# Row vectors loaded by GpSimd's queue, whole-row squares, and logits' copies shared by two engines, in a two-layer hybrid decoder

## The chip, the core and the metric

One core of a Trainium2 chip runs the whole program. The engines are TensorE (PE; PEld are its weight loads), VectorE (DVE), ScalarE (ACT), GpSimd (POOL) and SyncE (SP, which here only issues transfers). The metric is the device time of one execution in microseconds (us), the median over repeated runs.

## What is computed

Two layers, on 512 tokens of width 1024, in float32. Cut to what matters here:

```python
c_act = silu(c)
for l in range(2):
    mod = c_act @ w_ada[l] + b_ada[l]                 # 6 x 1024 numbers
    shift_m, scale_m, gate_m, shift_f, scale_f, gate_f = split(mod, 6)
    h = rms_norm(x, norm_mix[l]) * (1 + scale_m) + shift_m
    x = x + gate_m * mixer(h, w_in[l], ..., w_out[l])  # attention + gated linear attention
    h = rms_norm(x, norm_ffn[l]) * (1 + scale_f) + shift_f
    x = x + gate_f * moe(h, router, w_gate, w_up, w_down)  # 4 groups x 8 experts, top 2 of one group
```

`rms_norm(x, g)` is `x / sqrt(mean(x*x) + eps) * g`, row by row. The router's logits (36 a token) choose two of 32 experts for each token.

## The kernel before

**Layout.** The 512 tokens are four tiles of 128 rows (`tt` from 0 to 3), the width is eight slices of 128 columns (`k` from 0 to 7). Each layer is a mixer and then a mixture of experts (`moe`). A scheduler orders the instructions of each engine when the program is built; `kept_dma`, `pm` and `keep_in_program_order` fix the order of some of them. A tile's place in a pool is handed out again when its last reader is done, and whoever writes it next waits for that. SP's transfers take eight completion semaphores in turn, so that the ninth in flight waits for the first to land.

**The program's beginning.** SP loads c, the four tiles of `x`, and then `rows`: 100 short rows of 512 B (parts of `b_ada`, the two norm gains, `b_gk`) in seven transfers. Behind them come the modulation's weights. `ada` (L217 on) makes one of the six vectors, 256 columns at a time: two loads `wada` of 512 KB, 8 products on PE, a copy `row` on ACT (L245), a small transpose `adaT`, and on DVE the additions of `modulation` (L263 to L266) with the vectors of `cols`, which are `rows` transposed by PE (L198) and copied by DVE (L199). For each pair of slices k two such vectors are needed (scale, then shift): four loads `wada`, followed by two loads `raw` of `w_in`. PE transposes the normed x (`hT`, L364); DVE makes `hf` from it with the modulation (L366); ACT and DVE split it into a high and a low part (`hh`, `hl`, L95 and L96), and `raw` into `whl` in the same way; PE multiplies them (`proj`, L74). Ahead of that, ACT squares x in half rows of 512 columns with a running sum (`square`, L272), `inv_rms` makes the four columns `rs`, and DVE scales x by them, 1024 columns at a time (L347).

**The way from a mixer to its experts.** `logits` (L844 on) turns the finished x with four transposes a slice (`xT`, L849), DVE copies each slice out of PSUM (L851), and PE multiplies it with the router's weights (`lgT`), even slices into one half of the partitions and odd slices into the other. ACT writes the four normed tiles `xn` (L898), which GpSimd's queue stores to DRAM (`xg`); DVE's chain of comparisons ends in the list `idx` (L972), and GpSimd's indirect transfers fetch the listed rows (L977) for the first expert. The tiles `xn` have four places. The first lies where a load buffer of the mixer was, the second where `logits` keeps its slices `xT`.

**Experts.** For each pair of experts PE runs `gu`, `d` and `y`; the weights stream in through SP (`wgu`, `wd`), in the order of a `queue`.

Of the kernel before, what the change touches and what calls it, by code (L numbers as in the profile page):

```python
# [9 lines left out]
F = mybir.dt.float32  # L10
R = mybir.dt.float32r
BF = mybir.dt.bfloat16
I32 = mybir.dt.int32
U32 = mybir.dt.uint32
AF = mybir.ActivationFunctionType
OP = mybir.AluOpType
# [3 lines left out]
D, S, L = 1024, 512, 2  # L20
P = 128
NT, KT = S // P, D // P
# [7 lines left out]
def hybrid_decoder_kernel(ctx, tc, x, c, w_ada, b_ada, norm_mix, norm_ffn, w_in, w_gk2, b_gk, q_gain,  # L30
# [4 lines left out]
    tiny = ctx.enter_context(tc.tile_pool(name="tiny", bufs=2))  # L35
    dram = ctx.enter_context(tc.tile_pool(name="dram", bufs=1, space=bass.MemoryType.DRAM))
    V, A, G, T, SY = nc.vector, nc.scalar, nc.gpsimd, nc.tensor, nc.sync

    def slots(pool, tag, bufs, size):
        def get(shape, dt=F, name=None):  # L40
            n = 2 if dt == BF else 4
            for d in shape[1:]:
                n *= d
            assert n <= size, (tag, shape)
            return pool.tile(shape, dt, name=name or tag, tag=tag, bufs=bufs)
        return get
# [14 lines left out]
    def bank(name, tag, bufs, shape=None):  # L61
        return psum[1].tile(shape or [P, 512], F, name=name, tag=tag, bufs=bufs)
# [4 lines left out]
    def att(name="att"):  # L67
        return bank(name, "att", 3)

    def misc(name="misc", shape=None):  # L70
        return bank(name, "misc", 1, shape)

    def mm(o, a, b, start, stop):
        T.matmul(o, a, b, start=start, stop=stop, skip_group_check=True)  # L74

    def pm(o, a, b, start, stop):

        tc.keep_in_program_order(T.matmul(o, a, b, start=start, stop=stop, skip_group_check=True))  # L78
# [7 lines left out]
    def kept_dma(eng, o, a):  # L86

        tc.keep_in_program_order(eng.dma_start(o, a))

    def along(src, offset, n):  # L90

        return bass.AP(tensor=src.tensor, offset=src.offset + offset, ap=[[0, P], [1, n]])
# [37 lines left out]
    ident = const.tile([P, P], F, name="ident")  # L130
# [56 lines left out]
    def load_rows():  # L187

        rows = rowt[0]([100, P], name="rows")
        for l in range(L):  # L190
            for i in range(2):
                r = 32 * l + 16 * i
                kept_dma(SY, rows[r:r + 16], b_ada[l, 3 * D * i:3 * D * i + 2 * D].rearrange("(r p) -> r p", p=P))
        kept_dma(SY, rows[64:80], norm_mix.rearrange("l (k p) -> (l k) p", p=P))
        kept_dma(SY, rows[80:96], norm_ffn.rearrange("l (k p) -> (l k) p", p=P))
        kept_dma(SY, rows[96:100], b_gk.rearrange("l (g p) -> (l g) p", p=P))
        ps = misc("cols")
        T.transpose(ps[:, 0:100], rows, ident[0:100, 0:100])  # L198
        V.tensor_copy(cols, ps[:, 0:100])  # L199
# [23 lines left out]
    def ada(l, c0, n, raw, bank, at, later=True):  # L223

        vec, half = c0 // D, c0 % D // 512
        src = w_ada[l].rearrange("(p k) n -> p k n", k=KT)
        product = pm if later else mm
        ws, m = {}, 1024 // n
        for k in range(0, KT, m):
            w = raw([P, m, n], name="wada")  # L230
            (SY.dma_start if later else lambda *a: kept_dma(SY, *a))(w, src[:, k:k + m, c0:c0 + n])
            for i in range(m):
                ws[k + i] = w[:, i]
            if later and k % 4 == 2:
                yield
        if later and vec in (2, 5) and not half:
            gates[l, vec] = (gts if vec == 5 else gms[l])([P, D])
            kept_dma(G, gates[l, vec], along(b_ada, l * 6 * D + vec * D, D))
        yield
        row = rowt[at]([P, n], name="row")  # L240

        ps = bank("ada")
        for k in range(KT):
            product(ps[32 * (k % 4):32 * (k % 4) + 32, 0:n], ct1[:, k:k + 1].to_broadcast([P, 32]), ws[k], k < 4, k >= 4)
        A.copy(row, ps[:, 0:n])  # L245
        yield
        if vec in (2, 5):
            ps = bank("adaG")
            product(ps, sel, row, True, True)
            g = gates[l, vec][:, 512 * half:512 * half + 512]  # L250
            V.tensor_tensor(g, ps, g, op=OP.add)
        else:
            ps = bank("adaT")
            for i in range(n // P):
                product(ps[:, i:i + 1], row[:, P * i:P * i + P], sel[:, 0:1], i == 0, True)
            modulation(l, vec, slice(c0 % D // P, (c0 % D + n) // P), ps)
        yield
# [11 lines left out]
    def square(ss, xt, tt, q):  # L269

        junk = small([P, 512], BF, name="junk")
        A.activation(junk, xt[tt // 2][:, tt % 2, 512 * q:512 * q + 512], AF.Square, accum_out=ss[:, q, tt:tt + 1])  # L272
# [10 lines left out]
    def mixer(l, xt, ss, x_src, pool, later):  # L283
# [11 lines left out]
        s2 = slots(pool, "s2", 4, 2048)  # L295
# [9 lines left out]
        if l == 0:  # L305
            for k in range(0, KT, 2):
                first[k] = [ada(l, vec * D + P * k, 256, mixs, misc, l, False) for vec in (1, 0)]
            xt = [xq([P, 2, D], name="x") for _ in range(2)]
            for tt in range(NT):
                kept_dma(SY, xt[tt // 2][:, tt % 2], x_src[P * tt:P * tt + P, :])  # L310
            load_rows()
            for g in first[0]:
                next(g)
        wv = w_in[l].rearrange("(k p) n -> p k n", p=P)
# [11 lines left out]
        lrT = const.tile([RANK, S], F, name="lrT", tag="lrT")  # L326


        if l == 0:
            for tt in range(NT):  # L330
                for q in range(2):
                    square(ss, xt, tt, q)
        if l:

            ps = att("warm")
            for _ in range(16):
                pm(ps[:, 0:P], ident, ident, True, True)
        pin = tiny.tile([P, 1], F, name="pin")
        A.copy(pin, ss[:, 0, 0:1])
        tc.keep_in_program_order(A.preload_act_table_set("natural_log_exp_and_others"))  # L340
        rs = inv_rms(ss, G if l else A)
        xn = []
        for tt in range(NT):
            t = xt[tt // 2][:, tt % 2]
            xn.append(t if l == 0 else mixs([P, D], name="xn"))
            if l == 0:
                V.tensor_scalar(xn[tt], t, rs[:, tt:tt + 1], None, op0=OP.mult)  # L347
            else:
                V.tensor_scalar(xn[tt][:, 0:512], t[:, 0:512], rs[:, tt:tt + 1], None, op0=OP.mult)
                A.activation(xn[tt][:, 512:D], t[:, 512:D], AF.Copy, scale=rs[:, tt:tt + 1])  # L350
        if l:

            for i in range(2):
# [433 lines left out]
        ss = tiny.tile([P, 2, NT], F, name="ss")  # L787
# [53 lines left out]
    def logits(l, xt, s2):  # L841


        wr, lc, _ = route[l]  # L844
        lgT = misc("lgT")
        for k in range(KT):
            ps = att("xT")
            for tt in range(NT):
                T.transpose(ps[:, P * tt:P * tt + P], xt[tt // 2][:, tt % 2, P * k:P * k + P], ident)  # L849
            t = s2([P, S], name="xT")  # L850
            V.tensor_copy(t, ps)  # L851
            o = 64 * (k % 2)
            mm(lgT[o:o + 64], wr[:, 36 * k:36 * k + 64], t, k < 2, k >= KT - 2)
        t = s2([P, S], name="lgT")
        V.tensor_copy(t, lgT)
        lg = route[l][2] = att("lg")[:, 0:NT * 36].rearrange("p (t e) -> p t e", t=NT)
        for tt in range(NT):
            mm(lg[:, tt], t[:, P * tt:P * tt + P], two_parts, tt == 0, True)

    def moe(l, xt, ss, pool):  # L860
        wgu = slots(pool, "wgu", 5, 16384)
        wd = slots(pool, "wd", 4, 8192)
        g4 = slots(pool, "gT", 3, 4096)
        rows_ = slots(pool, "rows", 4, 4096)
        ot = slots(pool, "o", 2, 2048)
        ohl = slots(pool, "ohl", 4, 2048)
        ohs = slots(pool, "ohT", 1, 2048)
        s2 = slots(pool, "s2", 2, 2048)
        s1 = slots(pool, "s1", 4, 1024)

        queue = [(0, 0), (0, 1), (0, 2), (0, 3), (1, 0), (1, 1), (0, 4), (1, 2), (1, 3)]
        for i in range(0, NE, 2):
            queue += [(0, e) for e in (i + 5, i + 6) if e < NE] + [(1, e) for e in (i + 4, i + 5) if e < NE]
        loaded = {}
# [18 lines left out]
        wr, lc, lg = route.pop(l)  # L893
        rs = inv_rms(ss)

        for tt in range(NT):
            xn = rows_([P, KT, P], name="xn")
            normed = A.activation(xn, xt[tt // 2][:, tt % 2].rearrange("t (p k) -> t k p", k=KT), AF.Copy,  # L898
                                  scale=rs[:, tt:tt + 1])
            kept_dma(G, xg[P * tt:P * tt + P, :], xn.rearrange("t k p -> t (k p)"))  # L900

        def t3(n, name, dt=F):
# [25 lines left out]
        _, ge, gi, go = first_max(lo[:, :, 0:4], 4, "g")  # L928
# [5 lines left out]
        m1, _, i1, o1 = first_max(sl, 8, "a")  # L934
        s2nd = t3(8, "s2nd")
        V.scalar_tensor_tensor(s2nd, o1, -3.0e38, sl, op0=OP.mult, op1=OP.add)
        m2, _, i2, _ = first_max(s2nd, 8, "b")
# [206 lines left out]
        def overflow_lists():  # L1144
# [38 lines left out]
                                                 op=OP.is_equal))  # L1183
# [130 lines left out]
    xt, ss = None, tiny.tile([P, 2, NT], F, name="ss")  # L1314
    for l in range(L):
        if l:
            psum_pool(f"psum_mixer{l}")
        with tc.tile_pool(name=f"mixer{l}", bufs=1, reuse_waits="tile") as pool:
# [10 lines left out]
            xt, ss = mixer(l, xt, ss, x[0] if l == 0 else xs[:, :], pool, later)  # L1329
# [36 lines left out]
```

## Time and profile before

| | |
|---|---|
| time, median of 3 runs (lowest to highest) | 1230.94 us (1230.35 to 1233.77) |
| profiled execution: its time, its span | 1231.71 us, 1229.6 us |
| PE, DVE, ACT, POOL busy, share of the span | 96%, 56%, 38%, 15% |
| mean rate of the transfers | 254 GB/s |

The span is the time from the first to the last instruction that the profiler saw; the execution's own time is 2.1 us longer. The share of an engine is an average over stages with quite different limits.

### The profile page before, as it was taken

Reading aid. Unit: us, or ns where it says so; the run is one execution under the profiler, and the core shown is the slowest. Engines: PE = TensorE matmul, PEld = TensorE weight load, DVE = VectorE, ACT = ScalarE, POOL = GpSimd, SP = SyncE. Lnnn points to the kernel's source line nnn. Section 1 sums busy time; section 2 is a strip of 40 time slices with the busy share of each in tenths; the row PEclk is TensorE's granted clock in tenths of the full one; section 3 lists DMA queues with packets and bytes.
Section 4 is the critical chain, followed back from the end, with each engine's and each line's share of the span. In section 5 each row is a group of like instructions: output and inputs, shape, how many; then the busy total and the mean of one; then the engine's idle time right before and its main releaser. Section 6 shows DMA issues by size and latency. Waiting matters only on the chain. (4 is left out here: it accounts for less than half of the span.)

```text
span 1229.6 us, 17212 instructions
## 1 busy us (share of the span) xinstructions
PE 1176.4 (96%) x6441; PEld 743.4 (60%) x6441; DVE 687.8 (56%) x1343; ACT 472.6 (38%) x940; POOL 188.2 (15%) x222
## 2 busy tenths in 40 slices
PE   4999999999989999999999997999999999999996
PEld 2687766666765444444478785666776744444443
DVE  4475545465864555555566563445846565555553
ACT  4376646453242111111155764454624411111111
POOL 1000010011302222221110001001310222222110
PEclk8999999999999999999999999999999999999999
DMA  9653665643687999999445354564129599999981
GB/s 299 211 181 110 202 166 155 198 152 96 258 353 265 410 411 420 420 419 418 178 168 167 96 172 108 171 179 127 56 103 383 212 397 420 420 418 420 420 328 69
DMA packets 105902, 312.27 MB, mean 254 GB/s; under 512 B 12852, under 2 KB 49912, under 8 KB 81240
## 3 DMA queue, kind: packets, MB, share of 16 engines
q1 hardware_dynamic: 96920, 289.62, 63.3%
q0 software_dynamic: 8896, 21.52, 5.2%
q8 instruction: 52, 0.85, 0.3%
q14 instruction: 34, 0.28, 0.1%
HBM read 311.08 MB, written 8.40 MB: 260 GB/s over the span
## 5 line engine op out<-in xcount | busy, mean ns | idle before, releaser
L78 PE MATMUL gu<-wgu,gT 128*64 128x512 f32 x1024 | 225.4, 592 | 0.1
L74 PE MATMUL proj<-whl,hh 128*128 128x512 f32 (+2 forms) x768 | 220.6, 370 | 0.1
L78 PEld LDWEIGHTS gu<-wgu,gT 128*64 128x64 f32 x1024 | 75.4, 137 | 143.7 <-issue 142.2
L74 PEld LDWEIGHTS proj<-whl,hh 128*128 128x128 f32 x768 | 133.9, 190 | 35.0 <-issue 13.3
L1070 DVE TENSOR_TENSOR x<-y,x 128x512 f32<-128x512 f32 x240 | 148.2, 679 | 0.9 <-PE y L78 0.9
L74 PE MATMUL proj<-whl,hl 128*128 128x512 f32 (+2 forms) x384 | 138.6, 362 | 0.0
L1025 DVE TENSOR_TENSOR hs<-hs,gu 128x256 f32<-128x256 f32 x32 | 13.5, 421 | 201.2 <-ACT hs L1024 201.2
L78 PE MATMUL d<-wd,hT 128*64 128x512 f32 x512 | 116.9, 598 | 1.4 <-ACT hT L1034 1.4
L1063 POOL TENSOR_TENSOR olo<-o,ohi 128x512 fp32r<-128x512 f32 x60 | 77.0, 1285 | 263.4 <-ACT ohi L1062 263.4
L96 DVE TENSOR_TENSOR whl<-raw,whl 128x512 fp32r<-128x512 f32 (+2 forms) x128 | 73.2, 574 | 78.0 <-ACT whl L95 67.6
L78 PE MATMUL y<-ohi,oT 128*128 128x512 f32 x240 | 104.5, 436 | 0.0
L95 ACT ACTIVATE whl<-raw 128x512 fp32r<-128x512 f32 (+2 forms) x128 | 66.4, 524 | 76.6 <-PE proj L74 64.7
L78 PE MATMUL y<-olo,oT 128*128 128x512 f32 x240 | 94.2, 393 | 0.0
L74 PEld LDWEIGHTS proj<-whl,hl 128*128 128x128 f32 x384 | 72.4, 189 | 14.2 <-issue 4.3
L1024 ACT ACTIVATE hs<-gu 128x256 f32<-128x256 f32 x32 | 12.3, 385 | 168.4 <-PE gu L78 168.4
L78 PEld LDWEIGHTS d<-wd,hT 128*64 128x64 f32 x512 | 33.9, 136 | 62.2 <-issue 48.1
L78 PEld LDWEIGHTS y<-ohi,oT 128*128 128x128 f32 x240 | 45.4, 189 | 31.7 <-issue 26.0
L1003 ACT ACTIVATE gT<-g,mod 128x256 f32<-128x256 f32 (+1 forms) x72 | 39.0, 544 | 62.6 <-DVE gT L1005 62.3
L1062 ACT ACTIVATE ohi<-o 128x512 fp32r<-128x512 f32 x60 | 37.8, 630 | 61.7 <-DVE o L1057 61.7
L1057 DVE SCALAR_TENSOR_TENSOR o<-d,cws,gate_f 128x512 f32<-128x512 f32 x64 | 47.6, 746 | 21.4 <-PE d L78 21.4
L733 POOL TENSOR_TENSOR raw<-raw,gate_m 128x1024 f32<-128x1024 f32 x16 | 40.4, 2533 | 122.9 <-DMA raw<-in_w_out_dram 63.1
L78 PE MATMUL ada<-wada,ct 128*32 128x512 f32 x320 | 50.2, 600 | 5.3 <-DMA wada<-in_w_ada_dram 3.8
(332 smaller groups left out, 1935.0 us busy)
## 6 DMA issues: line engine op xcount, KB each, us to landing
wgu<-in_w_gate_dram SPq DMA_DIRECT2D x64, 1024.0 KB, 9.6
wgu<-in_w_up_dram SPq DMA_DIRECT2D x64, 1024.0 KB, 11.8
wd<-in_w_down_dram SPq DMA_DIRECT2D x64, 1024.0 KB, 11.0
wada<-in_w_ada_dram SPq DMA_DIRECT2D x96, 512.0 KB, 5.1
raw<-in_w_in_dram SPq DMA_DIRECT2D x80, 256.0 KB, 4.5
raw<-in_w_out_dram SPq DMA_DIRECT2D x16, 512.0 KB, 5.0
raw<-in_w_in_dram SPq DMA_DIRECT2D x32, 128.0 KB, 4.0
xg<-xn POOLq DMA_DIRECT2D x8, 512.0 KB, 5.9
```

Source lines behind the costliest of these rows:

```text
L74: T.matmul(o, a, b, start=start, stop=stop, skip_group_check=True)
L78: tc.keep_in_program_order(T.matmul(o, a, b, start=start, stop=stop, skip_group_check=True))
L95: A.activation(hi, src, AF.Copy)
L96: eng.tensor_tensor(lo, src, hi.bitcast(F), op=OP.subtract)
L733: G.tensor_tensor(t, t, gates[l, 2][:, None, cols].to_broadcast([P, 2, 512]), op=OP.mult)
L1003: A.activation(o, src, AF.Identity, scale=m, bias=b)
L1024: A.activation(hs[r], gu[r, 0:256], AF.Silu)
L1025: V.tensor_tensor(hs[r], hs[r], gu[r, 256:512], op=OP.mult)
L1057: V.scalar_tensor_tensor(o, pd, cws[:, i:i + 1], gate, op0=OP.mult, op1=OP.mult)
L1062: A.activation(hi, o, AF.Copy)
L1063: (G if last is None else V).tensor_tensor(lo, o, hi.bitcast(F), op=OP.subtract)
L1070: V.tensor_tensor(xc, ps, xc, op=OP.add)
```

## The change

- **Beginning.** The seven loads of `rows` are issued by GpSimd's queue, before its other loads; SP goes from `x` straight to `wada`. The squares are taken over whole rows of 1024 columns, the second column of sums being set to zero. The normed x is made half by DVE and half by ACT, as layer 1 does already. After the third tile's sum PE runs one product of one element that waits for it, and 12 products of the identity with itself, which nothing reads.
- **Logits.** Odd slices are copied by ACT, even ones by DVE.
- **Normed rows.** Tile 3 goes first and is made by GpSimd; tiles 0 to 2 by ACT. The pool of their places is named one line earlier. In `queue` the fifth expert's `wgu` comes before the first two `wd`.

```diff
@@ load_rows
-                kept_dma(SY, rows[r:r + 16], b_ada[l, 3 * D * i:3 * D * i + 2 * D].rearrange("(r p) -> r p", p=P))
-        kept_dma(SY, rows[64:80], norm_mix.rearrange("l (k p) -> (l k) p", p=P))
...
+                kept_dma(G, rows[r:r + 16], b_ada[l, 3 * D * i:3 * D * i + 2 * D].rearrange("(r p) -> r p", p=P))
+        kept_dma(G, rows[64:80], norm_mix.rearrange("l (k p) -> (l k) p", p=P))
...
@@ mixer
+            load_rows()
             xt = [xq([P, 2, D], name="x") for _ in range(2)]
             for tt in range(NT):
                 kept_dma(SY, xt[tt // 2][:, tt % 2], x_src[P * tt:P * tt + P, :])
-            load_rows()
...
+        pin = tiny.tile([P, 1], F, name="pin")
         if l == 0:
+            V.memset(ss[:, 1], 0.0)
             for tt in range(NT):
-                for q in range(2):
-                    square(ss, xt, tt, q)
+                junk = s2([P, D], BF, name="junk")
+                A.activation(junk, xt[tt // 2][:, tt % 2], AF.Square, accum_out=ss[:, 0, tt:tt + 1])
+                if tt == 0:
+                    A.copy(pin, ss[:, 0, 0:1])
+                    tc.keep_in_program_order(A.preload_act_table_set("natural_log_exp_and_others"))
+
+        ps = att("warm")
+        if l == 0:
+            pm(ps[0:1, 0:1], ss[:, 0, 2:3], ident[:, 0:1], True, True)
+        for _ in range(16 if l else 12):
+            pm(ps[:, 0:P], ident, ident, True, True)
...
-            if l == 0:
-                V.tensor_scalar(xn[tt], t, rs[:, tt:tt + 1], None, op0=OP.mult)
-            else:
-                V.tensor_scalar(xn[tt][:, 0:512], t[:, 0:512], rs[:, tt:tt + 1], None, op0=OP.mult)
-                A.activation(xn[tt][:, 512:D], t[:, 512:D], AF.Copy, scale=rs[:, tt:tt + 1])
+            V.tensor_scalar(xn[tt][:, 0:512], t[:, 0:512], rs[:, tt:tt + 1], None, op0=OP.mult)
+            A.activation(xn[tt][:, 512:D], t[:, 512:D], AF.Copy, scale=rs[:, tt:tt + 1])
@@ logits
-            V.tensor_copy(t, ps)
+            (A.copy if k % 2 else V.tensor_copy)(t, ps)
@@ moe
+        rows_ = slots(pool, "rows", 4, 4096)
         wd = slots(pool, "wd", 4, 8192)
         g4 = slots(pool, "gT", 3, 4096)
-        rows_ = slots(pool, "rows", 4, 4096)
...
-        queue = [(0, 0), (0, 1), (0, 2), (0, 3), (1, 0), (1, 1), (0, 4), (1, 2), (1, 3)]
+        queue = [(0, 0), (0, 1), (0, 2), (0, 3), (0, 4), (1, 0), (1, 1), (1, 2), (1, 3)]
...
-        for tt in range(NT):
+        for tt in (3, 0, 1, 2):
...
+            if tt == 3:
+                tc.keep_in_program_order(G.tensor_tensor(xn, src, rs[:, tt:tt + 1, None].to_broadcast([P, KT, P]), op=OP.mult))
+            else:
+                normed = A.activation(xn, src, AF.Copy, scale=rs[:, tt:tt + 1])
```

The built program shows three places at which the order moves. The first is SP's queue at the program's beginning. Before:

```order
L185 DMA cT<-in_c_dram 128x8
L88 DMA x<-in_x_dram 128x1024 x4
L88 DMA rows<-in_b_ada_dram 16x128 x4
L88 DMA rows<-in_norm_mix_dram 16x128
L88 DMA rows<-in_norm_ffn_dram 16x128
L88 DMA rows<-in_b_gk_dram 4x128
L88 DMA wada<-in_w_ada_dram 128x4x256 x4
L403 DMA raw<-in_w_in_dram 128x2x256 x2
```

And of the change:

```order
L185 DMA cT<-in_c_dram 128x8
L88 DMA x<-in_x_dram 128x1024 x4
L88 DMA wada<-in_w_ada_dram 128x4x256 x4
L406 DMA raw<-in_w_in_dram 128x2x256 x2
L88 DMA wada<-in_w_ada_dram 128x4x256 x4
L406 DMA raw<-in_w_in_dram 128x2x256 x2
```

The seven loads of `rows` are gone from this queue, and stand on GpSimd's before its four loads of `gain`.

The second place is ACT's queue, from `rs` to the first `hh`. Before:

```order
L103 ACTIVATE newton<-sm 128x4
L104 ACTIVATE rs<-newton 128x4
L245 COPY row<-ada 128x256 x2
L95 ACTIVATE whl<-raw 128x512
L95 ACTIVATE hh<-hf 128x512 x2
```

And of the change:

```order
L103 ACTIVATE newton<-sm 128x4
L104 ACTIVATE rs<-newton 128x4
L353 ACTIVATE x<-x,rs 128x512 x4
L95 ACTIVATE whl<-raw 128x512 x2
L245 COPY row<-ada 128x256 x2
L95 ACTIVATE hh<-hf 128x512
```

Four halves of the normed x come in, and the two splits of `raw`, which need its loads, now stand ahead of the two copies `row`.

The third place is PE's queue in `logits`. Before:

```order
L849 MATMUL xT<-ident,x 128x128 x12
L74 MATMUL lgT<-xT,wr 64x512 x2
L849 MATMUL xT<-ident,x 128x128 x4
L74 MATMUL lgT<-xT,wr 64x512 x2
L849 MATMUL xT<-ident,x 128x128 x12
L74 MATMUL lgT<-xT,wr 64x512 x2
L849 MATMUL xT<-ident,x 128x128 x3
L74 MATMUL lgT<-xT,wr 64x512
L849 MATMUL xT<-ident,x 128x128
L74 MATMUL lgT<-xT,wr 64x512
```

And of the change:

```order
L852 MATMUL xT<-ident,x 128x128 x12
L74 MATMUL lgT<-xT,wr 64x512 x3
L852 MATMUL xT<-ident,x 128x128 x10
L74 MATMUL lgT<-xT,wr 64x512
L852 MATMUL xT<-ident,x 128x128 x6
L74 MATMUL lgT<-xT,wr 64x512 x3
L852 MATMUL xT<-ident,x 128x128 x4
L74 MATMUL lgT<-xT,wr 64x512
```

The eight products stand in groups of 3, 1, 3 and 1 where they stood in groups of 2, 2, 2, 1 and 1.

## Rows read from the trace of the kernel before

**Rows 1.** The page's first part: busy time, share, instructions.
```profile
PE 1176.4 (96%) x6441; PEld 743.4 (60%) x6441; DVE 687.8 (56%) x1343; ACT 472.6 (38%) x940; POOL 188.2 (15%) x222
```
**Rows 2.** Windows: stretch, length, busy by engine, PE's clock, DMA share, GB/s.
```profile
3.00:13.00 10.00, 0.27 (x1) 0.18 (x1) 2.83 (x21) 7.62 (x21) 3.48 (x9) 1.00 0.89 297
13.00:22.00 9.00, 6.72 (x49) 3.18 (x48) 3.88 (x11) 0.94 (x5) 0.00 (x0) 1.00 1.04 345
23.00:29.00 6.00, 5.16 (x19) 2.94 (x19) 3.99 (x6) 1.78 (x3) 0.00 (x0) 0.50 1.10 349
30.00:35.00 5.00, 5.00 (x36) 3.10 (x36) 0.49 (x3) 1.29 (x4) 0.00 (x0) 1.00 1.08 343
```
**Rows 3.** Timelines of SP's and of POOL's issues at the beginning: start, duration, what.
```profile
1.20 1.84 SPq L88 DMA_DIRECT2D x<-in_x_dram  x4
...
10.54 2.21 SPq L88 DMA_DIRECT2D wada<-in_w_ada_dram  x4
12.79 1.40 SPq L403 DMA_DIRECT2D raw<-in_w_in_dram  x2
...
1.98 1.31 POOL L320 DMA_DIRECT2D gain<-in_q_gain_dram  x2
```
**Rows 4.** Transfers at 2.65, 4.9, 13.6 and 363.7 us: KB, us to landing.
```profile
x<-in_x_dram SPq DMA_DIRECT2D x1, 512.0 KB, 7.9
...
rows<-in_b_ada_dram SPq DMA_DIRECT2D x1, 8.0 KB, 6.8
wg<-in_w_gk_dram POOLq DMA_DIRECT2D x1, 16.0 KB, 6.7
...
raw<-in_w_in_dram SPq DMA_DIRECT2D x1, 256.0 KB, 7.8
...
xg<-xn POOLq DMA_DIRECT2D x1, 512.0 KB, 5.0
```
**Rows 5.** Timeline, 0 to 45 us: start, us, instruction, idle before and its releaser.
```profile
20.57 1.07 PE L74 MATMUL ada<-wada,ct 128*32 128x256 f32 x16 [0.25 <-DVE mod L263]
...
21.70 0.37 ACT L245 COPY row<-ada 128x256 f32<-128x256 f32 x1 [2.05 <-DMA wada<-in_w_ada_dram]
21.97 0.63 ACT L95 ACTIVATE whl<-raw 128x512 fp32r<-128x512 f32 x1
...
22.13 0.62 PE L74 MATMUL adaT<-sel,row 128*128 128x1 f32 x4 [0.49 <-ACT row L245]
...
22.98 1.53 DVE L366 TENSOR_SCALAR hf<-hT,mod 128x512 f32<-128x512 f32 x2
23.82 1.35 ACT L95 ACTIVATE hh<-hf 128x512 fp32r<-128x512 f32 x2 [1.22 <-DVE hf L366]
...
23.84 1.11 PE L364 MATMUL hT<-ident,x 128*128 128x128 f32 x4 [1.10 <-DVE hf L366]
...
24.61 1.20 PE L74 MATMUL proj<-whl,hh 128*128 128x512 f32 x2
```
**Rows 6.** Timeline, layer 0's logits and the way to its first expert.
```profile
346.27 1.67 PE L74 MATMUL lgT<-xT,wr 128*64 128x512 f32 x4
...
355.94 1.07 PE L74 MATMUL lgT<-xT,wr 128*64 128x512 f32 x2 [0.78 <-DVE xT L851]
...
357.05 6.25 ACT L898 ACTIVATE xn<-x,rs 128x1024 f32<-128x1024 f32 x3 [5.12 <-PE lgT L74]
...
363.59 0.53 POOL L88 DMA_DIRECT2D xg<-xn  x1 [1.52 <-ACT gd L1201]
...
368.14 0.17 DVE L972 TENSOR_SCALAR idx<-nv 128x16 int32<-128x16 f32 x1 [0.49 <-PE nv L78]
```
**Rows 7.** Timeline of POOL and of DVE, 305 to 345 us.
```profile
310.08 10.40 POOL L733 TENSOR_TENSOR raw<-raw,gate_m 128x1024 f32<-128x1024 f32 x4 [10.65 <-DMA raw<-in_w_out_dram]
...
311.27 0.69 DVE L746 TENSOR_TENSOR x<-op,x 128x512 f32<-128x512 f32 x1 [0.40 <-PE op L74]
...
314.77 6.26 DVE L96 TENSOR_TENSOR wl<-raw,wh 128x512 fp32r<-128x512 f32 x3
```

More of the change, by code (lines that the diff above doesn't have):

```diff
@@ L192, in load_rows @@
                 r = 32 * l + 16 * i
-                kept_dma(SY, rows[r:r + 16], b_ada[l, 3 * D * i:3 * D * i + 2 * D].rearrange("(r p) -> r p", p=P))
-        kept_dma(SY, rows[64:80], norm_mix.rearrange("l (k p) -> (l k) p", p=P))
-        kept_dma(SY, rows[80:96], norm_ffn.rearrange("l (k p) -> (l k) p", p=P))
-        kept_dma(SY, rows[96:100], b_gk.rearrange("l (g p) -> (l g) p", p=P))
+                kept_dma(G, rows[r:r + 16], b_ada[l, 3 * D * i:3 * D * i + 2 * D].rearrange("(r p) -> r p", p=P))
+        kept_dma(G, rows[64:80], norm_mix.rearrange("l (k p) -> (l k) p", p=P))
+        kept_dma(G, rows[80:96], norm_ffn.rearrange("l (k p) -> (l k) p", p=P))
+        kept_dma(G, rows[96:100], b_gk.rearrange("l (g p) -> (l g) p", p=P))
         ps = misc("cols")
@@ L326, in mixer @@
         lrT = const.tile([RANK, S], F, name="lrT", tag="lrT")
+        pin = tiny.tile([P, 1], F, name="pin")
         if l == 0:
+            V.memset(ss[:, 1], 0.0)
             for tt in range(NT):
-                for q in range(2):
-                    square(ss, xt, tt, q)
-        if l:
[L335 to L340, printed above, removed]
+                junk = s2([P, D], BF, name="junk")
[8 more added lines that the diff above has]
+            pm(ps[:, 0:P], ident, ident, True, True)
+        if l:
+            A.copy(pin, ss[:, 0, 0:1])
+            tc.keep_in_program_order(A.preload_act_table_set("natural_log_exp_and_others"))
         rs = inv_rms(ss, G if l else A)
@@ L894, in moe @@
         rs = inv_rms(ss)
-        for tt in range(NT):
+        for tt in (3, 0, 1, 2):
             xn = rows_([P, KT, P], name="xn")
-            normed = A.activation(xn, xt[tt // 2][:, tt % 2].rearrange("t (p k) -> t k p", k=KT), AF.Copy,
-                                  scale=rs[:, tt:tt + 1])
+            src = xt[tt // 2][:, tt % 2].rearrange("t (p k) -> t k p", k=KT)
+            if tt == 3:
+                tc.keep_in_program_order(G.tensor_tensor(xn, src, rs[:, tt:tt + 1, None].to_broadcast([P, KT, P]), op=OP.mult))
+            else:
+                normed = A.activation(xn, src, AF.Copy, scale=rs[:, tt:tt + 1])
             kept_dma(G, xg[P * tt:P * tt + P, :], xn.rearrange("t k p -> t (k p)"))
```

## The prediction

> **What bounds the kernel.** I read the page's first part, then its execution cut into stretches. PE is busy for 96% of the span [rows 1], and from 30 us on for the whole of a stretch [rows 2]. So a microsecond off another engine is worth nothing, unless it lets PE start earlier, run at a higher clock, or do less. Two places are not like that. Up to 24.6 us, PE's first `proj` [rows 5], PE waits for the beginning: between 3 and 13 us it works 0.27 us, while the transfers have a share of 0.89 [rows 2]. The second is the way from the logits to the first expert, twice in the program, where engines wait for each other in turn [rows 6].
>
> At the beginning SP is done with `x` at 3.0 us, but its first `wada` is issued at 10.54 [rows 3]. The last of `x`, issued at 2.6, took 7.9 us, to 10.5 [rows 4]: with the seven loads of `rows` in the eight places in flight, `wada` waits for it. The second `raw`, issued at 13.45 (the two take from 12.79 to 14.19 [rows 3]), lands 7.8 us later, at 21.2 [rows 4]. I call that landing R. The row copy and the first split `whl` stand at 21.70 and 21.97, `hf` at 22.98, `hh` at 23.82, and the first `proj` at 24.61, thus R + 3.4 [rows 5].
>
> **The beginning, step by step.** With `rows` off SP's queue, four `wada` and two `raw` can follow `x` from 3 us on. They don't come earlier by as much: the bytes ahead of R are the same, and the transfers were not idle. What can be won is the unused share, set against the 1.10 that they reach later: 10 x (1.10 - 0.89) + 8.2 x (1.10 - 1.04) = 2.6 us [rows 2], so R lies between 18.6 and 21.2. One transfer of 512 KB of GpSimd's queue also moves back behind `rows`; if all of it fell behind R, 512 KB at 345 GB/s [rows 2] are 1.5 us more, R = 17.1. I take 2.0 us, R = 19.2, nearer to the full rate because the queue now always holds work.
>
> What follows R gets longer. ACT's order puts both `whl` ahead of both copies `row`, and they need R. So the scale vector's row, made of weights that have long landed, is copied only at R + 1.6 (two splits at 0.6 and a copy of 0.4) [rows 5]. Then `adaT` 0.6 on PE, R + 2.2; three transposes at 1.11/4 each, R + 3.0; the shift's 16 `ada` records, 1.07 at the full clock of their row [rows 5] and, as I estimate from that, 2.14 at half, R + 5.2; its row 0.4, `adaT` 0.6, R + 6.2. Behind that PE has a transpose, the next pair's first `ada` and four transposes ahead of `proj`: 0.14 + 1.07 + 0.55 at the full clock, R + 8.0. `mod` 0.2, `hf` 0.77 and `hh` 0.67 [rows 5] lie beside it. With the full clock from R on the same chain gives R + 6.3, with half throughout R + 9.7. Which holds is unknown: before, 23 to 29 us had clock 0.50 with PE busy 5.16 of 6 us, and 30 to 35 clock 1.00 [rows 2]. PE now waits longer just ahead of R and after it, so I take half up to R + 6.2 and full behind.
>
> To compare the two: before, PE ran at half clock from 24.6 to between 29 and 30 [rows 2, 5]. With 29.4 that is work of 2.4 us at full; it stands like a kernel that starts at 27.0 at the full clock. After, one `ada` vector (1.07) is done ahead of `proj` which before came behind it. So the starts are level at P = 28.1. My P is 19.2 + 8.0 = 27.2: **-0.9 us**. The bounds: R = 17.1 and the full clock, P = 23.4, -4.7; R = 21.2 and half throughout, P = 30.9, +2.8.
>
> The whole-row squares, the halves of the normed x (0.7 us each on two engines) and the 13 extra products lie ahead of R, in a stretch where ACT works 0.94 of 9 us, DVE 3.88 and PE 6.72 [rows 2]: nothing, while that cover lasts. A few transposes of x get later; PE has room for them ahead of R + 1.6.
>
> The seven loads cost GpSimd's queue seven issues of 0.6, from 1.98 on [rows 3], so the last one leaves at 5.5 to 6 and lands 6.7 us later [rows 4], at 12.5. PE's first instruction needs them (`cols`), and DVE's copy of it stands ahead of the last steps of `rs`. From there about 7 us of work on DVE, ACT and PE must be over by R + 1.6 = 20.8: nothing is lost up to a landing at 13.9. A second wait: only eight of this queue's transfers are in flight too, so the later `gain` loads are now issued when the first `rows` land, 1.98 + 6.8 = 8.8 and behind, up to about 10, and land near 16.5. DVE's product for `gain` stands between two halves of the normed x, and behind it wait the halves of tiles 2 and 3 and all transposes. They need 0.2 + 1.4 + 1.1 us and must be done at R + 1.6: nothing up to about 18. Both are slack of 1.4 us, one for one behind it.
>
> For these landings the row is 6.7 us for `wg` of GpSimd's queue beside 6.8 for `rows` of SP's, issued within two microseconds [rows 4]: no difference between the queues. The Trainium skill, "SBUF — State Buffer", section "SBUF: two separate sides", says otherwise in its box on DVE blocking DMA: transfers that GpSimd issues have their descriptors written by GpSimd, which certain DVE operations lock out, and it advises SP's or ACT's queue; by it the sum would be that of rival 4 below. The trace does not bear it out so far, with DVE busy 2.83 of the 10 us around them [rows 2].
>
> **Logits.** PE's products come in groups of 3, 1, 3, 1. A group of two took 1.67, a single 1.07 [rows 6], so one more in a group is 0.6. Before: 3 x 1.67 + 2 x 1.07 = 7.15. After: 2 x 2.27 + 2 x 1.07 = 6.68. That is -0.47 a layer, bounds 0 (waits eat it; the last product already waits 0.78 for DVE's copy) and -0.9 (that wait shrinks too): **-1.0 us** for two layers.
>
> **Normed rows.** The same places serve in both programs, so the earlier pool decides nothing. GpSimd's tile has the place that is free early; ACT's three tiles begin with the place over `xT` and wait for the last product, as before (5.12 for `lgT`, then 6.25 for three [rows 6]). So the last `xg` is issued as late after the last product as now. It lands at 363.59 + 5.0 = 368.6, while `idx` is ready at 368.3 [rows 6]: at most 0.3 a layer hangs on it. The fifth `wgu` ahead of two `wd` shifts 1 to 2 us of loads that PE-bound experts hide. Together **-0.2 us**, 0 to -0.6. GpSimd's product of 128x1024 took 2.6 us elsewhere [rows 7], at most about 5 with a strided input; its tile is the first to be stored, so that is covered.
>
> **Sum.** -0.9 - 1.0 - 0.2 = -2.1 against the profiled execution's 1231.71 (span 1229.6 and 2.1 around it): 1229.6. The median of the runs is 0.77 below that execution, so the forecast of the median is **1228.8 us**. 0.3%, about what a measurement of this kernel can tell from no change, is 3.7 us.
>
> **Rivals.**
> 1. *The clock stays full at the beginning.* The 13 extra products could hold PE's clock over its wait. Then P = 19.2 + 6.3 = 25.5, -2.6, in all -3.8, and -4.4 with R = 18.6: about 1226.7. For it: 13 to 22 us had the full clock before with PE at 6.72 of 9. Against it: 23 to 29 did not, right behind [rows 2].
> 2. *The loads come no earlier*, so that the change does not do what moving `rows` suggests. Then R = 21.2, P = 29.2, +1.1, in all -0.1: 1230.8; with half clock throughout +2.8 and in all +1.6: 1232.5. For it: the share of 1.04 just ahead of R was already near full.
> 3. *Slower: GpSimd's product stops DVE's chain.* Three two-input operations of DVE took 6.26 us beside GpSimd's products, 2.1 each, whereas one that reads PSUM took 0.69 [rows 7]. If GpSimd's tile starts behind the last product, it stands in DVE's chain to `idx`, on which all waits: +2 to 2.6 a layer, so -0.9 - 1.0 + 5 = +3.1, 1234. It decides from a start later than `lgT`'s copy; before that, DVE only copies from PSUM. Against it: place, x and `rs` are there earlier.
> 4. *Slower: `rows` or `gain` land late.* Every microsecond behind 13.9 or 18 costs one. In all slower than now from 16.1 and 20.2, by over 3.7 us from 19.8 and 23.9. At twice the 6.7 us, 5.5 + 13.4 = 18.9: +2.9, 1233.8.
>
> **Chances.** The forecast's own case 0.48, from 1227.3 to 1230.3; rival 1 0.25, with 0.06 beside it for gains of several terms at their bounds; rival 2 0.12; rivals 3 and 4 0.05 and 0.04. Faster by over 3.7 us is most of rival 1, the 0.06 and a little of the forecast's: 0.33. Slower by over 3.7: the far ends of rivals 3 and 4 and of 2 at half clock: 0.07. Within: 0.60. The range 1225.0 to 1231.8 leaves out the best gains and about 0.12 above.
>
> **What would show it.** Right: first `wada` issued near 3 to 5 us, second `raw` landed at 18.6 to 19.5, first `proj` near 27 with half clock up to about 25; GpSimd's rows landed by 13; lgT's four groups 0.5 us shorter a layer; the last `xg` still 6.6 us after the last product. Wrong: full clock from 19 us on, R at 21, DVE's two-input operations of 2 us behind `lgT`, a wait for `gain` or `cols`, or a wait that a shorter beginning leaves to the loads behind it, since from 23 to 35 us their share is 1.08 to 1.10 and no more.

## The result, and the profile after

| kernel | median of its runs, us | median of the kernel before beside it, us | ratio, 95% interval |
|---|---|---|---|
| changed kernel | 1224.48 | 1230.94 | 0.9948 [0.9923, 0.9974] |
| the same, a second time | 1227.49 | 1231.30 | 0.9972 [0.9953, 0.9992] |
| the same, a third time | 1226.37 | 1232.73 | 0.9956 [0.9938, 0.9975] |

The change is faster by 0.28% to 0.52%, 3.4 to 6.4 us; the mean of the three ratios, 0.9959, is 5.1 us. The prediction said 2.1 us. Single executions of one kernel lie up to 15 us apart here (1221.67 to 1236.39 us for no_moe, a kernel of the experiments), so that a stage is read from traces below, and a whole kernel only from a ratio and its interval.

The profiled execution after has a time of 1228.59 us and a span of 1226.4. Its page and the four stretches of [rows 1, 2]; the columns are busy time by engine, PE's clock, DMA share and GB/s:

```profile
PE 1174.6 (96%) x6467; PEld 749.3 (61%) x6467; DVE 686.3 (56%) x1336; ACT 473.6 (39%) x942; POOL 196.7 (16%) x231
```

```profile
3.00:13.00 10.00, 1.94 (x10) 1.77 (x11) 3.56 (x25) 6.71 (x14) 7.16 (x16) 1.00 0.98 355
13.00:22.00 9.00, 5.28 (x39) 3.95 (x38) 1.63 (x6) 3.02 (x6) 0.00 (x0) 1.00 1.07 336
23.00:29.00 6.00, 6.00 (x39) 3.75 (x43) 1.60 (x7) 0.37 (x1) 0.00 (x0) 0.50 0.91 296
30.00:35.00 5.00, 5.00 (x37) 3.67 (x33) 1.36 (x5) 1.63 (x4) 0.00 (x0) 0.76 0.86 267
```

The unused share of the transfers between 3 and 13 us is filled as forecast (0.98 for 0.89), and then it falls: 0.91 and 0.86 where it was 1.10 and 1.08. PE runs at half clock there, and it looks as if the loads behind the beginning now wait for PE; the run row_first bears this out below.

The clock column needs care. The trace has records of PE's clock only from 19.2 us on before, and from 15.3 us on after; ahead of them the column shows 1.00 without a reading. Two rows of the kernel before show what the clock was:

```profile
16.23 1.08 PE L74 MATMUL ada<-wada,ct 128*32 128x256 f32 x8
18.08 1.08 PE L74 MATMUL ada<-wada,ct 128*32 128x256 f32 x8
```

Eight records of `ada` took 1.08 us here, as long as sixteen at 20.57 [rows 5]. So before, PE ran at half clock up to 19 us, at full clock from there to 22.6, and at half again to 29.4. Up to 19 us the 1.00 in [rows 2] is not what PE had.

SP's issues at the beginning, against [rows 3]:

```profile
3.08 2.60 SPq L88 DMA_DIRECT2D wada<-in_w_ada_dram  x4
5.73 6.49 SPq L406 DMA_DIRECT2D raw<-in_w_in_dram  x2
```

PE and ACT in the same stretch, against [rows 5]:

```profile
11.50 4.74 PE L78 MATMUL warm<-ident 128*128 128x128 f32 x24
16.17 1.07 PE L74 MATMUL ada<-wada,ct 128*32 128x256 f32 x16
...
22.62 1.01 PE L74 MATMUL adaT<-sel,row 128*128 128x1 f32 x4 [3.01 <-ACT row L245]
...
24.30 1.94 PE L74 MATMUL ada<-wada,ct 128*32 128x256 f32 x16
...
27.08 0.85 PE L74 MATMUL adaT<-sel,row 128*128 128x1 f32 x4
...
28.18 1.94 PE L74 MATMUL ada<-wada,ct 128*32 128x256 f32 x16
...
30.82 1.20 PE L74 MATMUL proj<-whl,hh 128*128 128x512 f32 x2
...
69.77 0.63 PE L493 MATMUL kT<-ident,two 128*128 128x128 f32 x4
```

```profile
21.16 1.15 ACT L95 ACTIVATE whl<-raw 128x512 fp32r<-128x512 f32 x2 [5.98 <-DMA raw<-in_w_in_dram]
22.21 0.35 ACT L245 COPY row<-ada 128x256 f32<-128x256 f32 x1
26.31 0.37 ACT L245 COPY row<-ada 128x256 f32<-128x256 f32 x1 [3.74 <-PE ada L74]
```

The first `wada` is issued at 3.1 instead of 10.5, and the first `ada` is done at 17.2. Yet its row is copied at 22.2: ACT stands 5.98 us at `whl`, which waits for the second `raw`, landed at 21.1. PE's `adaT` waits 3.01 us for that copy, `ada` takes 1.94 instead of 1.07, and `proj` starts at 30.8, R + 9.7. Here the chain of the prediction can be followed entry by entry. `kT`, a transpose of a later step of the mixer, serves below as the mark at which the beginning is over.

Layer 0's logits on PE, against [rows 6], after and then before (with PE's first `kT` before, the mark of the beginning, as its first row):

```profile
344.87 1.47 PE L852 MATMUL xT<-ident,x 128*128 128x128 f32 x12
346.42 1.93 PE L74 MATMUL lgT<-xT,wr 128*64 128x512 f32 x6
...
349.61 1.07 PE L74 MATMUL lgT<-xT,wr 128*64 128x512 f32 x2
...
351.42 1.93 PE L74 MATMUL lgT<-xT,wr 128*64 128x512 f32 x6
...
354.66 1.07 PE L74 MATMUL lgT<-xT,wr 128*64 128x512 f32 x2 [0.73 <-ACT xT L854]
356.52 1.08 PE L74 MATMUL lg<-two_parts,lgT 128*128 128x36 f32 x8 [0.78 <-DVE wr L825]
```

```profile
67.85 0.63 PE L490 MATMUL kT<-ident,two 128*128 128x128 f32 x4
...
344.73 1.47 PE L849 MATMUL xT<-ident,x 128*128 128x128 f32 x12
...
348.45 1.93 PE L74 MATMUL lgT<-xT,wr 128*64 128x512 f32 x4
...
351.77 1.65 PE L74 MATMUL lgT<-xT,wr 128*64 128x512 f32 x4
...
357.80 1.08 PE L74 MATMUL lg<-two_parts,lgT 128*128 128x36 f32 x8 [0.78 <-DVE wr L822]
```

From the first transpose to `lg` it is 11.65 us after and 13.07 before: 1.42 less, in each layer. The groups of two took 1.67, 1.93 and 1.65; a group of three takes 1.93, no more than the longest of them. All groups together are 7.39 before and 6.00 after.

GpSimd's rows behind it, with DVE's `idx` and the first product of the experts, after and then before:

```profile
348.64 2.44 POOL L903 TENSOR_TENSOR xn<-x,rs 128x1024 f32<-128x1024 f32 x1 [27.92 <-DVE rs L109]
...
362.30 0.53 POOL L88 DMA_DIRECT2D xg<-xn  x1 [1.51 <-ACT gd L1207]
367.98 0.17 DVE L978 TENSOR_SCALAR idx<-nv 128x16 int32<-128x16 f32 x1 [1.57 <-PE nv L78]
368.44 1.43 POOL L983 DMA_INDIRECT rows<-xg,idx  x1 [5.61 <-DVE e L1213]
...
374.38 7.16 PE L78 MATMUL gu<-wgu,gT 128*64 128x512 f32 x32
```

```profile
369.58 1.09 POOL L977 DMA_INDIRECT rows<-xg,idx  x1 [5.46 <-DVE den L1212]
...
375.15 7.16 PE L78 MATMUL gu<-wgu,gT 128*64 128x512 f32 x32
```

Before, `idx` was ready at 368.31 and the fetch was issued 1.27 us later; after, at 368.15, it follows by 0.29. In layer 1 it was 0.78 before and is 1.25 after.

### The profile page after: what moved, and what is told of

It is laid out like the page before. It is cut to its first block, busy times and chain, and to the rows that moved or that the text cites. A ratio compares the mean times of both kernels' runs of the same rounds, so it can differ in the third digit from the quotient of the medians.

```text
span 1226.4 us, 17270 instructions
## 1 busy us (share of the span) xinstructions
PE 1174.6 (96%) x6467; PEld 749.3 (61%) x6467; DVE 686.3 (56%) x1336; ACT 473.6 (39%) x942; POOL 196.7 (16%) x231
## 4 chain that ended last, share of the span: by engine, by line
PE 85%; DMA 6%; DVE 5%; ACT 2%; issue 1%; SPq 1%; DVEq 0%; ACTq 0%
PE proj L74 19%; PE gu L78 18%; PE y L78 10%; PE d L78 9%; PE op L74 6%; PE z L74 5%; DMA wada<-in_w_ada_dram 3%; PE ada L78 3%; PE g L1003 2%; DMA raw<-in_w_in_dram 2%; PE warm L78 1%; PE pv L74 1%; PE lgT L74 1%; PE o L74 1%; PE adaT L78 1%
## 5 line engine op out<-in xcount | busy, mean ns | idle before, releaser
L95 ACT ACTIVATE whl<-raw 128x512 fp32r<-128x512 f32 (+2 forms) x128 | 66.6, 524 | 85.1 <-PE proj L74 66.9
L78 PEld LDWEIGHTS d<-wd,hT 128*64 128x64 f32 x512 | 33.9, 136 | 62.2 <-issue 48.1
```

Of the source, the lines that this page charges most:

```text
L95: A.activation(hi, src, AF.Copy)
```

## The experiments

A stage is given for layer 0 and layer 1 of one profile each. "Stage" is the time from the first transpose of `logits` to the first product `gu` of the experts: 30.42 and 30.12 us before.

**The whole change again.** No edit.

> The changed kernel once more. Theory A (the step from the ledger of the two profiles): the gain is logits' shorter groups, 1.4 us a layer, of which half is lost again on the way to the first expert, and nothing from the beginning; then the median is 1.5 to 3.5 us under the kernel before, and the first median's 6.5 us was partly spread. Theory B (rival 1 of the prediction): in the faster executions PE's clock stays full at the beginning, and the 6.5 us are real; then the median is 5 to 8 us under, and a profiled execution near 1223 us shows the clock at half for under 5 us between 15 and 35 us, where the first profile showed it for 10.2.

Measured: 0.9972 [0.9953, 0.9992], 3.4 us, the upper end of theory A. Its profiled execution was a long one (span 1232.2): with the same instructions, PE waited for a load `wada` in it, and its clock was at half from 157.6 to 167.8 us. The first two rows are of this run, the third of the first profile:

```profile
158.87 1.92 PE L78 MATMUL ada<-wada,ct 128*32 128x512 f32 x4 [3.99 <-DMA wada<-in_w_ada_dram]
```

```profile
150.00:170.00 20.00, 16.01 (x67) 9.43 (x65) 3.13 (x9) 4.71 (x10) 4.17 (x7) 0.74 0.94 217
```

```profile
150.00:170.00 20.00, 19.64 (x115) 12.54 (x113) 9.21 (x19) 10.55 (x21) 4.16 (x7) 1.00 0.89 216
```

Against the first profile, this run is 0.3 us behind at PE's first `kT` and 7.0 us behind at 188 us, and stays so. Such falls are one cause of the spread of single executions. One other of the 17 profiles has it, that of no_moe (a wait of 3.60 us, half clock from 158.3); no other waits longer than 1.63 us there. Both have the new beginning, so that a part of the change in it can't be ruled out. The clock at the beginning did not stay full (half up to 34.7 us): theory B has nothing for it. Theory A's stage is there: 28.66 and 28.11.

**Each part alone**, on the kernel before.

```diff
# begin_only: load_rows and the part of mixer, as in the change
# logits_only:
-            V.tensor_copy(t, ps)
+            (A.copy if k % 2 else V.tensor_copy)(t, ps)
# moe_only: the pool's line, the queue and the normed rows, as in the change
```

> Only the beginning is changed (rows on GpSimd's queue, whole-row squares, halves of the normed x, the 12 products). Theory A: PE's first kT comes 1.5 to 2.5 us later than before, the loads of the mixer take that back by 240 us, and the time is the same, within 1 us of before. Theory B: 3 to 5 us faster than before.

> Only the copies of logits are on two engines. Theory A: PE's lgT groups are 3, 1, 3, 1 and sum to 6.0 us where they were 7.4; from the first transpose xT to lg 1.4 us less in each layer; up to 1.1 of it lost again where 12 extra products at half clock stand ahead of nv; in all 0.8 to 2.8 us faster. Theory B: the same, since it only speaks of the beginning.

> Only the normed rows, the pool and the queue of loads are changed. Both theories: idx at the same time after the last lgT as before; the last xg lands up to 1.5 us earlier after it is issued, and the fetch follows idx by 0.3 to 0.5 us where it was 1.3 in layer 0 and 0.8 in layer 1: 0.5 to 1.3 us faster; the prediction's own term was 0.2.

Measured: 1.0000 [0.9979, 1.0021], 0.9991 [0.9973, 1.0009] and 0.9991 [0.9977, 1.0005]. The beginning alone brings nothing that can be told from 0, within 2.6 us: theory A. Its `kT` came at 66.9, not later than before, since PE's clock was back at full from 26.4 us on; where it falls and rises differs from execution to execution. In logits_only the way from transpose to `lg` is 11.65 in both layers, as foreseen, and its stage 28.93 and 28.61. In moe_only the stage is 30.00 and 30.28, and the fetch follows `idx` by 0.28 in both layers. The other two intervals reach over 1 as well. The three ratios add up to 2.2 us, less than the whole change, though by less than their intervals together allow. By stages, the logits alone save 3.0 us in two layers and the normed rows alone 0.3. One reason why they are worth more together shows in logits_only, where the odd copies `xT` fill ACT ahead of its normed rows, all four of which now come behind the last odd copy:

```profile
352.42 8.30 ACT L898 ACTIVATE xn<-x,rs 128x1024 f32<-128x1024 f32 x4
```

With GpSimd's tile there are three (6.23 us after). In logits_only the last `xg` is issued 6.58 us behind `lg`, in the whole change 5.78, and the fetch comes 1.14 and 1.42 us behind `idx`.

**Each part left out** of the changed kernel.

```diff
# no_begin: load_rows and mixer as before
# no_logits:
-            (A.copy if k % 2 else V.tensor_copy)(t, ps)
+            V.tensor_copy(t, ps)
# no_moe: the pool's line, the queue and the normed rows as before
```

> The changed kernel with the beginning of the kernel before. Theory A (logits and normed rows carry the gain, the beginning nothing): 3 to 5.5 us under the kernel before, as the whole change. Theory B (the parts add up as they measured alone): 1 to 2.5 us under.

> The changed kernel with logits' copies all on DVE again. Theory A: 1.5 to 3.5 us slower than the whole change, thus 1 to 2.5 us under the kernel before, and from the first xT to lg 1.4 us longer in each layer. Theory B: 1 us under the kernel before.

> The changed kernel with the normed rows and the queue of loads as before. Theory A: 1 to 2.5 us slower than the whole change, 2.5 to 4 us under the kernel before; the fetch follows idx by 0.8 to 1.3 us again. Theory B: 1 us under the kernel before.

Measured: 0.9952 [0.9935, 0.9970], 0.9976 [0.9958, 0.9994] and 0.9967 [0.9948, 0.9986]. Without the beginning the gain is whole, 5.9 us, and its stage is 28.40 and 28.12: 4.0 us less in two layers, where logits and normed rows alone had 3.0 and 0.3. Without the logits' copies 3.0 us are left, without the normed rows 4.1 (the fetch then follows `idx` by 0.85 and 2.57), so that 2 to 3 us are missing beside no_begin on the same chip. For no_begin theory B is out: its 1 to 2.5 us lie below the interval of 3.7 to 8.0. The intervals of the last two reach over the whole change's, so they agree with theory A, but the share of each is not known better than that.

**The order behind R** (run row_first, and once more as rf_again; again2 is the changed kernel beside it). Orders are fixed at the beginning of the changed kernel: both copies `row` ahead of `whl` on ACT, and on PE the products of slice 0 ahead of the next pair's `ada`, which is written behind them.

```diff
-        A.copy(row, ps[:, 0:n])
+        a = A.copy(row, ps[:, 0:n])
+        if not later:
+            tc.keep_in_program_order(a)      # the same for whl's A.activation
...
-        product = pm if later else mm
+        product = pm
...
-                        mm(o, a, m, k == 0 and j == 0, k == KT - 1 and j == 2)
+                        (pm if lead and k < 2 else mm)(o, a, m, k == 0 and j == 0, k == KT - 1 and j == 2)
...
-            while n_prep < min(len(steps), i + ahead_prep + 1):
+            while n_prep < min(len(steps), i + ahead_prep + (l > 0 or i > 0)):
```

> The changed kernel with three orders fixed at the beginning: ACT makes both copies row ahead of the splits whl, PE the 12 products proj of slice 0 ahead of the next pair's ada, which is written behind them. Theory A (the order behind R costs what the chain says): the scale's adaT no longer comes 1.5 us after the second raw's landing R but before it, the first proj stands at R + 1.5 to 2.5 instead of R + 7.8 to 9.7, PE's first kT comes 2 to 4 us earlier than in the changed kernel, and the time falls by 1.5 to 4 us. Theory B (the loads bound this stretch anyway, and later waits for loads take back what it wins): first proj as early, but kT no more than 1 us earlier, and the time within 1 us of the changed kernel's.

> row_first once more: 6 to 10 us under the kernel before, and 2 to 5 us under the changed kernel on the same chip.

> The changed kernel a third time, beside row_first on the same chip. From the two comparisons so far (6.5 and 3.8 us under the kernel before): 3 to 6 us under it. Its adaT for the scale stands 1.5 us behind R again, and its first proj at R + 7.5 to 9.8.

Measured: 0.9937 [0.9915, 0.9958] and 0.9932 [0.9911, 0.9953], medians of 1218.71 and 1224.27 us where the kernel before had 1228.21 and 1232.73; the changed kernel beside the second, 0.9956. So row_first is 7.7 and 8.4 us faster than the kernel before, and faster than the changed kernel on the same chip by 2.1 us by the medians, by 3.0 by the ratios; the intervals of these two overlap a little. PE in row_first:

```profile
17.53 0.61 PE L78 MATMUL adaT<-sel,row 128*128 128x1 f32 x4
...
20.01 0.61 PE L78 MATMUL adaT<-sel,row 128*128 128x1 f32 x4
...
22.91 0.49 PE L78 MATMUL proj<-whl,hh 128*128 128x512 f32 x1
...
62.23 0.63 PE L499 MATMUL kT<-ident,two 128*128 128x128 f32 x4
```

and its stretch from 25 us on, with that of the changed kernel under it:

```profile
25.00:35.00 10.00, 10.00 (x84) 6.50 (x83) 3.88 (x9) 3.14 (x7) 0.00 (x0) 1.00 1.10 348
```

```profile
25.00:35.00 10.00, 10.00 (x70) 6.25 (x62) 3.36 (x8) 2.63 (x6) 0.00 (x0) 0.63 0.84 270
```

With R at 21.0, as late as in the changed kernel, both `adaT` lie ahead of it, `proj` starts at R + 1.9, PE's clock is at full from 15 us on, and `kT` comes at 62.2 instead of 69.8. This time the transfers are the ones in full use (1.10). That speaks for theory A: the order costs what the chain says. Of 7.5 us at `kT`, 2 to 3 are left at the end. The two profiles of one chip show where the lead goes: rf_again is 6.5 us ahead of again2 at `kT`, 6.9 at layer 0's first `xT`, and 1.7 at layer 1's. Between these two points, where the two kernels are the same, and where all 17 profiles take 589 to 598 us, the lead shrinks by 5.2 in this pair. That may be spread of single executions as well as a loss; no run settles it. In again2, R is 19.6, `adaT` starts at 21.1 and `proj` at 27.8, as expected.

**The extra products, and the queue, with that order and without.**

```diff
# no_extra (on the changed kernel) and rf_no_extra (on row_first):
-        for _ in range(16 if l else 12):
+        for _ in range(16 if l else 0):
# rf_rows_sp: row_first with rows loaded by SP behind x, as before
# rows_only, squares_only: on the kernel before, load_rows alone and the part of mixer alone
```

> The changed kernel without the 12 products that nothing reads (the one-element product stays). Theory A (they only fill PE's wait): first ada at the landing of its second load, about 12.5 instead of 16, everything from R on as in the changed kernel, the time the same within 1 us. Theory B (they hold PE's clock over the wait): half clock begins before 20 us and lasts longer than 10 us, 1 to 3 us slower.

> row_first without the 12 products that nothing reads; the order behind them stays, as a fixed one. Theory A (the order alone made row_first fast): first proj at R + 1.5 to 2.5, PE's first kT within 1.5 us of row_first's 62.2, the time within 1 us of row_first. Theory B (the products hold PE's clock at the full level over the wait): the clock is at half for more than 5 us between 15 and 35 us, kT comes 2 to 4 us later, and the time is 1.5 to 3 us more.

> row_first with the seven loads of rows back on SP's queue. Theory A (with the order fixed, earlier loads pay): R back at 21.2 to 22.3, kT 1 to 2 us later than in row_first, and the time 1 to 2 us more. Theory B (the mixer's later loads take it back): kT as much later, but by 240 us level with row_first but for the clock, and the time within 1 us.

> The kernel before with the seven loads of rows on GpSimd's queue and nothing else. Its order on ACT has one row, two whl, one row. Theory A: R between 19.5 and 21.1 instead of 21.2 to 22.3, the first proj at R + 5 to 6 since only the second row copy stands behind the splits; the time within 1.5 us of before. Theory B (loads alone set the beginning): R 1 to 2 us earlier and the time 1 to 2 us less.

> The kernel before with whole-row squares, the halves of the normed x and the 12 products; rows stay on SP's queue. Its order on ACT has both rows ahead of whl, as before. Both theories: R as before (21.2 to 22.3), first proj at R + 3 to 4.5, the time within 1 us of before.

Measured: no_extra 0.9987 [0.9974, 1.0000], rf_no_extra 0.9949 [0.9931, 0.9967], rf_rows_sp 0.9966 [0.9949, 0.9983], rows_only 1.0004 [0.9987, 1.0021], squares_only 0.9990 [0.9974, 1.0006]. no_extra tells its theories apart badly: without the products the scheduler puts one of the two `row`, the scale's, ahead of `whl` by itself (ACT makes it at 15.1, the two `whl` at 19.2, the other `row` at 20.8), so that two things change at once (first `proj` 25.1, `kT` 67.6). rf_no_extra, with the order fixed, is the clean one: `kT` at 65.0, 2.8 us later than row_first, and its first products take twice as long:

```profile
24.76 1.20 PE L78 MATMUL proj<-whl,hh 128*128 128x512 f32 x2
25.76 0.63 PE L78 MATMUL proj<-whl,hl 128*128 128x512 f32 x1
```

Its clock is at half up to 27.8 us. So the 12 products raise PE's clock (theory B). What this is worth in the whole time is less sure: 2.1 us by the two ratios of that chip, 1.2 by the medians, and the intervals overlap. The queue: with `rows` on SP, `kT` comes at 64.9, and the time is 4.2 us more than row_first's by the ratios of that chip, 2.3 by the medians: theory A, with the size between 2 and 4 us. R was 21.3, hardly later; what came later is the second vector's `wada`, and with it the second `adaT`, at 21.95 instead of 20.01. On the kernel before, the same move brings nothing (rows_only): first `proj` at 26.4, 1.75 us later than before, with PE at half clock up to 33.4. squares_only has both `row` ahead of `whl`, as expected, and is 1.2 us faster by its ratio, whose interval reaches over 1. Its trace shows more than was expected: PE's clock is at full from 16.7 us on, and `kT` comes 2.5 us earlier than before:

```profile
65.30 0.63 PE L493 MATMUL kT<-ident,two 128*128 128x128 f32 x4
```

This sets apart what row_first changes at once. At its beginning rf_rows_sp differs from squares_only by the fixed orders alone, and both have the two `row` first; its `kT`, 64.9, is only 0.4 earlier. So with `rows` on SP the fixed orders add little to what ACT's order does by itself; with `rows` on GpSimd's queue no run sets PE's order apart from ACT's. With the 12 products and both `row` first the earlier loads move `kT` from 65 to 62; where the same move puts `whl` first, `kT` goes to 67 to 70.

## Why the prediction was wrong

The sign of the whole was right, and so were two of the three places. The first measurement, 1224.48, lies 0.5 us under the range; the later two, set against the median before, would lie inside it. What failed are sizes, of each of the three terms, the logits' most of all:

- **The beginning, -0.9.** The chain behind R was right: `adaT` at R + 1.5 (said: 1.6), first `proj` at R + 9.7 with half clock throughout, the bound that was named. R = 19.2 was too hopeful in the first profile (21.1; 19.6 in the other two), and half clock lasted to 32 us, not 25. So the first profile is the slow bound of the prediction's own sum (P = 30.9; `proj` came at 30.8). Over six profiles with the new beginning and the logits or experts of either kind, `kT` comes at 66.9 to 70.0, in the mean 68.7; over four with the old one at 66.6 to 67.9, mean 67.1. So by traces the term is +1.5, and by begin_only 0 within 2.6 us. The unused share of the transfers was won, as said; the order that the scheduler chose, and the half clock in its wait, gave it back. The prediction had that order in its chain; what it took too high there was the clock. That the forecast was not further off is luck: its -0.9 for the beginning, which did not come, made up for part of what the other two terms lacked.
- **Logits, -0.5 a layer.** The failed step is "one more in a group is 0.6". It came from one group of two (1.67) and a single (1.07); another group of two in the same stage took 1.93, and that is what a group of three takes as well. In the prediction's own terms its sum was 7.15 before and 6.68 after, where the rows give 7.39 and 6.00. Measured from the first transpose to `lg`: -1.42 a layer, 11.65 in all eleven profiles with the new copies beside 13.07 in the six with the old (in row_first's layer 1 the first rows are missing). The wait of 0.78 stayed, at 0.73.
- **Normed rows, -0.2.** "At most 0.3 a layer hangs on it" compared the landing of `xg` with `idx` and did not look at the fetch, which stood in the trace 1.27 us behind `idx`. It follows now by 0.28 in the best case; over the profiles with the old code of this part it was 0.78 to 2.57, with the new 0.28 to 1.27. The mean is 0.7 less at the fetch (0.4 in the changed kernel's own three profiles, in all of which layer 1 has 1.25), part of it lost before `gu`. By the stage, the term is -0.1 a layer on the kernel before (moe_only) and -0.5 behind the new logits (28.93 and 28.61 in logits_only, 28.40 and 28.12 in no_begin): the prediction added the two terms as if one did not change the other, and the logits' odd copies on ACT move the normed rows. These are single profiles, and with both parts old the stage lies between 29.7 and 31.1, so that the sizes by the stage are not firm.

Together the stage is shorter by 1.6 us a layer in the mean of the three profiles of the whole change (29.50 and 29.20, 28.66 and 28.11, 28.59 and 28.05), 3.2 in all, where the prediction had 1.2. In no_begin it is 4.0. Between that and the 5.1 us of the ratios stay 1 to 2 us, inside the intervals, which no run has assigned.

In the first profile the stage is longest because of a wait that the prediction had not named. PE's clock was at half from 363.5 us on (before, the half clock of this stage began at 360.5, under products that nobody waits for), and 12 of the products that nothing reads stood at that clock ahead of `nv`:

```profile
363.65 3.23 PE L78 MATMUL warm<-lo,ident 128*128 128x144 f32 x12
366.81 1.12 PE L78 MATMUL nv<-exn,ohp 128*64 128x16 f32 x32
```

That is 1.1 us from `rk` to `nv` (3.52 for 2.44). It occurs in 4 of the 22 layers profiled with the new logits and in none of the 12 with the old.

Rival 1 (full clock at the beginning) did not come true for the changed kernel: half clock is in all its three profiles, up to 32, 35 and 33 us. It is what row_first, rf_again, rf_rows_sp and squares_only have. What the prediction said for this rival, that 13 to 22 us had the full clock before, was in the main a misreading: up to 19 us PE was at half clock there. Rival 2 (loads no earlier) is nearest to the first profile, R = 21.1. Rivals 3 and 4 did not happen: GpSimd's tile was done at 351.1, before `lgT` was copied, and `rows` landed at 11.0, `gain` at 18.2. That one reached its limit of 18, and DVE waited for it:

```profile
18.28 0.15 DVE L321 TENSOR_SCALAR gain<-gain 128x1 f32<-128x1 f32 x1 [4.78 <-DMA gain<-in_k_gain_dram]
```

It cost nothing only because `adaT` came later still. On the queue: seven loads issued by GpSimd took 4.8 to 5.6 us to land, less than the 6.8 of SP's row [rows 4], beside DVE at 3.56 of 10 us. The delay that the Trainium skill, "SBUF — State Buffer", section "SBUF: two separate sides", warns of does not show in these landings; whether any of DVE's operations beside them is of the kind that its box names, no run tells.

## What to carry to other kernels

Loads that come earlier are worth what stands next in the consumer's queue: here a copy whose data had long been there stood behind a split that waited for another load, and only with that order fixed did the new queue pay (2 to 4 us instead of 0). For the end of a wait, read the row of the instruction that waits, not the arrival of what one thinks it waits for. Take a group's price from all groups of its kind in the stage, not from one. And where a column shows full clock, check it by the time that a known instruction took.

## What the runs showed of the hardware

Products that nothing reads paid by their clock: `proj` took 1.20 a pair without and 0.62 with the 12 products, though these had ended 7 us ahead of it. They did so only where PE had no long wait behind them. In the four profiles with these products and both `row` first, the clock stays at full from 15 to 17 us on; in the six with `whl` first PE waits 3.0 to 5.4 us for a `row`, and the clock is at half for 3.4 to 13.7 us from 20 to 23 us on. The Trainium skill, "TensorE: Matmul & The Clock Gate", section "HAM oscillation — how this bites in real kernels", says that waits for transfers between bursts of work let the clock drop, and advises to order the loop so that PE stays warm; row_first, with no such wait behind 23 us, agrees (1.00 from 15 us on), and the changed kernel, with 3.01 us of wait at 22.6, too (0.50). The clock also fell where the program is dense otherwise, at 158 us in two of the six profiles with the new beginning (the second of the changed kernel, and no_moe). In these two PE had waited 3.99 and 3.60 us for a load `wada`; why that load came late is open.
